# A gated unit over 8192 rows: eight neighbouring rows for a partition in groups of four tiles, in place of four in groups of two

## The chip, the cores and the metric

The kernel runs on one core of one Trainium2 chip. The metric is the device time of one execution in microseconds (us), with all inputs and outputs in the chip's memory (HBM); smaller is better. A core has 128 partitions of on-chip memory. Data come in and go out by DMA: a program's transfers are cut into packets, and 16 DMA engines work on these. In this kernel three engines compute: ScalarE (ACT in the profile), VectorE (DVE) and GpSimd (POOL). SyncE (SP) and ScalarE issue the transfers. TensorE does nothing. KB and MB of tiles and of distances in memory are counted here in powers of 1024, those of the profile's totals (268.44 MB) in powers of 1000.

## The reference

```python
def setup_inputs():
    return {
        "x": np.random.randn(8192, 8192).astype(np.float32),
    }

def reference(x: np.ndarray) -> np.ndarray:
    a, b = np.split(x, 2, axis=-1)
    return a * (1 / (1 + np.exp(-b)))
```

Each row of x holds 4096 values of a and then 4096 of b. The output row has the 4096 products of a and the sigmoid of b. A row of x takes 32 KB, a row of the output 16 KB. 268.44 MB are read and 134.22 MB written, and each byte is used once.

## The kernel before, in words

The 8192 rows are cut into 32 tiles of 256 rows; each of the 128 partitions holds R = 2 rows of a tile (64 KB of x, 32 KB of output). Lines 21 and 22 say which rows these are. With `"(g p h r) m -> g h p (r m)"` and h=2, a group g of two tiles covers 512 neighbouring rows; partition p takes four neighbouring rows of them, and tile h of the group gets two of the four. So the piece of x that a partition loads for one tile is 64 KB without a break, and the next partition's piece lies 128 KB further on (the other tile's 64 KB are between them). For the output the piece is 32 KB and the pitch from partition to partition 64 KB.

There are SLOTS = 2 input buffers `x_sb0`, `x_sb1` of 128 x 16384 float32 (8 MB each) and two output buffers `o_sb0`, `o_sb1` of 128 x 8192 float32 (4 MB each), used in turn: tile i uses slot i % 2. All instructions stand in program order on their engine (`place` keeps the waits that are needed and declares the others away):

- `load` (line 59) issues from SP's queue one transfer for the whole tile (line 63); for tile 0 there are two, a row each, `rows = [(0, 4), (4, 8)]`. A load into a slot waits for the products that read the slot two tiles before.
- `work` (line 72) does the sigmoid in place on ScalarE (line 82) and then the product of both halves (line 84), cut into two pieces for tiles 1 to 30: a part of 2 x 768 columns, whose product GpSimd makes (VectorE for tile 1), and a part of 2 x 3328 columns, whose product VectorE makes. Tiles 0 and 31 are done in four quarters on VectorE. For tiles 1 to 30 the sigmoid carries the wait for the output slot: it starts when the store of two tiles before has landed.
- `store` (line 66) issues from ScalarE's queue one transfer for the tile (line 68); tile 0 has two and tile 31 three.

The loop (lines 91 to 103) loads tiles 0 and 1 ahead; then for each tile it does the work, issues the load of tile i + 2 and the store of tile i. `_launch_early` moves the first load into the entry block, ahead of the barrier there, and `_close_on_sync` writes the end of the program by hand; the change does not touch these two.

The change touches lines 18 to 22 (the layout), 63 (in `load`) and 68 (in `store`), the only places that hold the group's size.

Of the kernel before, what the change touches and what calls it, by code (L numbers as in the profile page):

```python
# [8 lines left out]
def _tiles(ctx, tc, x, out):  # L9
    nc = tc.nc  # L10
    P = nc.NUM_PARTITIONS
    DEP = mybir.DependencyInfo(mybir.DependencyClass.Sync, mybir.DependencyReason.DATA)
    fp32 = mybir.dt.float32
    SIG = mybir.ActivationFunctionType.Sigmoid

    n_rows, n_cols = x.shape
    half = n_cols // 2
    R = 2
    SLOTS = 2
    n_tiles = n_rows // (P * R)  # L20
    x_g = x.rearrange("(g p h r) m -> g h p (r m)", p=P, h=2, r=R)
    out_g = out.rearrange("(g p h r) m -> g h p (r m)", p=P, h=2, r=R)

    pool = ctx.enter_context(tc.tile_pool(name="io", bufs=1))
    xs = [pool.tile([P, R * n_cols], fp32, name=f"x_sb{k}") for k in range(SLOTS)]
    os = [pool.tile([P, R * half], fp32, name=f"o_sb{k}") for k in range(SLOTS)]

    whole = [(0, 8)]
    rows = [(0, 4), (4, 8)]
    cut = half // 16 * 3  # L30
    few_and_most = [(0, 8, 0, cut), (0, 8, cut, half)]
    fourths = [(k, k + 2, k % 4 * half // 4, (k % 4 + 2) * half // 4) for k in range(0, 8, 2)]
    loads = [whole] * n_tiles
    works = [few_and_most] * n_tiles
    stores = [whole] * n_tiles
    behind = [0] * n_tiles
    loads[0] = stores[0] = rows
    works[0] = works[-1] = fourths
    stores[-1] = [(0, 4), (4, 6), (6, 8)]
    behind[-1] = 1  # L40

    def meet(a, b):
        return a[0] < b[1] and b[0] < a[1]

    traced = [[] for _ in range(SLOTS)]
    load_of, mul_of, store_of = {}, {}, {}

    def place(i, ins, *needs):


        kept = {n.ins.name for n in needs}
        for e in traced[i % SLOTS]:
            if e.ins.name not in kept:
                tc.declare_no_dep(ins.ins, e.ins, reason="follows from the waits that are kept")
        traced[i % SLOTS].append(ins)
        tc.keep_in_program_order(ins)
        return ins

    def load(i):
        for lo, hi in loads[i]:  # L60
            c = slice(lo * n_cols // 4, hi * n_cols // 4)
            free = [m for w, m in mul_of.get(i - SLOTS, []) if meet(w, (lo, hi))]
            ins = nc.sync.dma_start(out=xs[i % SLOTS][:, c], in_=x_g[i // 2, i % 2, :, c])  # L63
            load_of.setdefault(i, []).append(((lo, hi), place(i, ins, *free)))

    def store(i, lo, hi):
        c = slice(lo * half // 4, hi * half // 4)
        ins = nc.scalar.dma_start(out=out_g[i // 2, i % 2, :, c], in_=os[i % SLOTS][:, c])  # L68
        done = [m for w, m in mul_of[i] if meet(w, (lo, hi))]
        store_of.setdefault(i, []).append(((lo, hi), place(i, ins, *done)))  # L70

    def work(i, lo, hi, near, far):

        rows = xs[i % SLOTS].rearrange("p (r h m) -> p r h m", r=R, h=2)
        packed = os[i % SLOTS].rearrange("p (r m) -> p r m", r=R)
        r, c = slice(lo // 4, (hi + 3) // 4), slice(near, far)
        b = rows[:, r, 1, c]
        landed = [s for w, s in load_of[i] if meet(w, (lo, hi))]
        gone = [s for w, s in store_of.get(i - SLOTS, []) if meet(w, (lo, hi))]
        by_sigmoid = 0 < i < n_tiles - 1  # L80
        needs = [*landed, *(gone if by_sigmoid else ())]
        sig = place(i, nc.scalar.activation(out=b, in_=b, func=SIG), *needs)  # L82
        engine = nc.gpsimd if far == cut and i > 1 else nc.vector
        mul = engine.tensor_mul(out=packed[:, r, c], in0=rows[:, r, 0, c], in1=b)  # L84
        if by_sigmoid:
            for s in gone:
                tc.add_manual_dep(sig.ins, s.ins.name, DEP, reason="frees the output slot")
        place(i, mul, sig, *(() if by_sigmoid else gone))
        mul_of.setdefault(i, []).append(((lo, hi), mul))

    for i in range(SLOTS):
        load(i)
    for i in range(n_tiles):
        due = list(stores[i])
        for k, piece in enumerate(works[i]):
            work(i, *piece)
            ready = works[i][k - behind[i]][1] if k >= behind[i] else 0
            while len(stores[i]) > 1 and k < len(works[i]) - 1 and due[0][1] <= ready:
                store(i, *due.pop(0))
        if i + SLOTS < n_tiles:  # L100
            load(i + SLOTS)
        for lo, hi in due:
            store(i, lo, hi)
# [71 lines left out]
@with_exitstack  # L175
def kernel(
    ctx: ExitStack,
    tc: tile.TileContext,
    x: bass.AP,
    out: bass.AP,  # L180
):
    nc = tc.nc
    with ExitStack() as pools:
        _tiles(pools, tc, x, out)
    tc.close()
    tc.compile()
    _launch_early(nc)
    _close_on_sync(nc)
# [30 lines left out]
```

## Time and profile before

| What | Value |
|---|---|
| Median of 3 runs | 932.84 us (932.70 to 932.84) |
| Span of the profiled execution | 931.1 us |
| VectorE busy | 232.5 us (25%) |
| ScalarE busy | 229.8 us (25%) |
| GpSimd busy | 99.9 us (11%) |
| Packets of the load queue (q1) | 4752, 268.44 MB |
| Packets of the store queue (q10) | 5040, 134.22 MB |
| Whole-tile load, issue to landing | 43.5 us, median of 31 |
| Whole-tile store, issue to landing | 43.6 us, median of 30 |

How to read it: the span is the time between the first and the last thing that the profiler saw of one execution; the median is 1.7 us longer than it. An engine's busy time is the sum of its instructions' durations; a transfer's time to landing counts from its issue and so includes the time in which its packets stand behind others. A packet here is one partition's unbroken piece, so a whole-tile load has 128 packets of 64 KB and a whole-tile store 128 of 32 KB; besides these, each of the 33 loads and 35 stores has 16 packets of 4 bytes that report completion (33 x 144 = 4752 and 35 x 144 = 5040).

### The profile page before, as it was taken

To read this page: it belongs to the slowest core of one execution; us is meant where nothing else is said; L and a number is where in the kernel's file an instruction comes from. 1 tells how busy PE (TensorE), PEld (TensorE's weight loads), DVE (VectorE), ACT (ScalarE), POOL (GpSimd) and SP (SyncE) were. 2 spreads that over 40 slices of the span, in tenths; PEclk is the share of its full clock that TensorE was granted. 3 is DMA by queue.
4 is the path that set the end of the run, shared out by engine and by line. 5 is a ranking of instruction groups with operands and counts; after the bars stand their busy time and mean duration, and the time that the engine had idled before them with its cause. 6 is when DMAs were issued, how large, how long until landed. Compare 5 with 4: busy or idle time off the path is not lost.

```text
span 931.1 us, 325 instructions
## 1 busy us (share of the span) xinstructions
DVE 232.5 (25%) x39; ACT 229.8 (25%) x69; POOL 99.9 (11%) x33
## 2 busy tenths in 40 slices
DVE  1133311333113331133320333203332033320233
ACT  2123332033320333203332023320233302333023
POOL 0001111011110111101111011110111101111010
DMA  9999999999999999999999999999999999999998
GB/s 405 450 439 417 428 450 424 455 405 428 450 428 450 407 469 409 428 450 427 452 405 450 428 428 450 424 452 408 428 450 428 450 408 465 411 428 450 427 452 383
DMA packets 9793, 402.67 MB, mean 432 GB/s; under 512 B 1088, under 2 KB 1088, under 8 KB 1088
## 3 DMA queue, kind: packets, MB, share of 16 engines
q1 hardware_dynamic: 4752, 268.44, 66.6%
q10 hardware_dynamic: 5040, 134.22, 33.4%
q14 instruction: 1, 0.01, 0.0%
HBM read 268.44 MB, written 134.22 MB: 432 GB/s over the span
## 4 chain that ended last, share of the span: by engine, by line
DMA 75%; DVE 12%; ACT 12%; issue 0%; ACTq 0%; SPq 0%
DMA out_dram<-o_sb 65%; DVE o_sb L84 12%; ACT x_sb L82 12%; DMA x_sb<-in_x_dram 10%; ACTq L68 0%; SPq L63 0%
## 5 line engine op out<-in xcount | busy, mean ns | idle before, releaser
L84 DVE TENSOR_TENSOR o_sb<-x_sb 128x6656 f32<-128x6656 f32 (+2 forms) x39 | 232.5, 5970 | 690.2 <-ACT x_sb L82 690.2
L82 ACT ACTIVATE x_sb<-x_sb 128x1536 f32<-128x1536 f32 (+1 forms) x68 | 228.5, 3407 | 689.9 <-DMA out_dram<-o_sb 630.0
L84 POOL TENSOR_TENSOR o_sb<-x_sb 128x1536 f32<-128x1536 f32 x29 | 99.7, 3437 | 787.7 <-ACT x_sb L82 787.7
L82 ACT ACT_TABLE_LOAD x1 | 1.3, 1283 | 0.8 <-PEq L203 0.8
L203 POOL MEMSET const-float32-0.0<- 128x1 f32 x1 | 0.1, 98 | 0.2 <-issue 0.2
L203 POOL MEMSET const-bfloat16-1.0<- 128x1 bf16 x1 | 0.1, 101 | 0.0
L203 POOL MEMSET const-uint8-127<- 128x1 uint8 x1 | 0.1, 101 | 0.0
L203 POOL MEMSET const-float32-1.0<- 128x1 f32 x1 | 0.1, 98 | 0.0
## 6 DMA issues: line engine op xcount, KB each, us to landing
out_dram<-o_sb ACTq DMA_DIRECT2D x30, 4096.0 KB, 43.6
x_sb<-in_x_dram SPq DMA_DIRECT2D x2, 4096.0 KB, 16.4
out_dram<-o_sb ACTq DMA_DIRECT2D x3, 2048.0 KB, 28.0
out_dram<-o_sb ACTq DMA_DIRECT2D x2, 1024.0 KB, 8.3
x_sb<-in_x_dram SPq DMA_DIRECT2D x31, 43.5
```

The costliest lines, as they stand in the source:

```text
L82: sig = place(i, nc.scalar.activation(out=b, in_=b, func=SIG), *needs)
L84: mul = engine.tensor_mul(out=packed[:, r, c], in0=rows[:, r, 0, c], in1=b)
L203: nc = _bacc.Bacc("TRN2", target_bir_lowering=False, num_devices=1)
```

## The change

The group becomes H = 4 tiles of 1024 neighbouring rows. Partition p takes eight neighbouring rows of a group, and each of the four tiles gets two of them. A partition's piece of a tile stays as it was, 64 KB of x and 32 KB of output; the pitch from one partition's piece to the next one's grows from 128 KB to 256 KB for loads and from 64 KB to 128 KB for stores. 8 groups take the place of 16. Nothing else is edited: the buffers, the instructions, their shapes and their order on every engine are the same, and the same row of the output comes from the same row of x.

```diff
     R = 2
+    H = 4
     SLOTS = 2
     n_tiles = n_rows // (P * R)
-    x_g = x.rearrange("(g p h r) m -> g h p (r m)", p=P, h=2, r=R)
-    out_g = out.rearrange("(g p h r) m -> g h p (r m)", p=P, h=2, r=R)
+    x_g = x.rearrange("(g p h r) m -> g h p (r m)", p=P, h=H, r=R)
+    out_g = out.rearrange("(g p h r) m -> g h p (r m)", p=P, h=H, r=R)
...
-            ins = nc.sync.dma_start(out=xs[i % SLOTS][:, c], in_=x_g[i // 2, i % 2, :, c])
+            ins = nc.sync.dma_start(out=xs[i % SLOTS][:, c], in_=x_g[i // H, i % H, :, c])
...
-        ins = nc.scalar.dma_start(out=out_g[i // 2, i % 2, :, c], in_=os[i % SLOTS][:, c])
+        ins = nc.scalar.dma_start(out=out_g[i // H, i % H, :, c], in_=os[i % SLOTS][:, c])
```

## The prediction, made before the changed kernel ran

> **What bounds the kernel now.** I read the busy shares first, then the DMA's share stage by stage, then the chain of waits, and last the packet records, one for each packet with its queue, bytes, start and duration. The page's busy rows, its row of DMA shares and its queues:
>
> ```profile
> DVE 232.5 (25%) x39; ACT 229.8 (25%) x69; POOL 99.9 (11%) x33
> ...
> DMA  9999999999999999999999999999999999999998
> ...
> q1 hardware_dynamic: 4752, 268.44, 66.6%
> q10 hardware_dynamic: 5040, 134.22, 33.4%
> ```
>
> No computing engine is busy for more than a quarter of the span. The 16 DMA engines are busy in every slice, and the two queues' packets fill 66.6% + 33.4% = 100% of 16 engines' span. The windows by stage (columns: window, length, busy time of DVE, ACT and POOL, TensorE's clock, DMA share, GB/s):
>
> ```profile
> 46.00:104.00 58.00, 15.94 (x3) 18.59 (x6) 6.22 (x2) 1.00 0.98 425
> 104.00:395.00 291.00, 70.92 (x10) 71.90 (x21) 35.05 (x11) 1.00 1.00 434
> 395.00:627.00 232.00, 56.74 (x8) 57.11 (x17) 27.48 (x8) 1.00 1.00 434
> 627.00:860.00 233.00, 56.74 (x8) 57.98 (x17) 27.49 (x8) 1.00 1.00 433
> 860.00:912.00 52.00, 14.18 (x2) 8.43 (x4) 3.43 (x1) 1.00 1.01 435
> 912.00:931.10 19.10, 8.99 (x4) 7.08 (x4) 0.00 (x0) 1.00 0.94 403
> ```
>
> The rate is flat at 433 to 435 GB/s, and only the two ends fall below it. The chain of waits in order of time (start, length, what) repeats one cycle:
>
> ```profile
> 113.99 43.64 DMA out_dram<-o_sb
> 157.63 0.02 issue
> 157.66 7.13 ACT x_sb L82 x2
> 164.79 0.02 issue
> 164.81 7.10 DVE o_sb L84
> 171.91 0.02 issue
> 171.93 0.02 ACTq L68
> 171.95 0.04 issue
> 171.99 43.64 DMA out_dram<-o_sb
> ```
>
> A cycle is 171.99 - 113.99 = 58.00 us for two tiles, 2 x 12.58 MB (in millions of bytes; a third of it stores), so 25.17 / 58.00 = 434 GB/s. The chain names a store's landing, but those 43.64 us are mostly queueing, as the packet records show: on an engine packets of loads and stores alternate, a 64 KB load packet for 2418 ns, then a 32 KB store packet for 1213 ns. Eight pairs, the share of one engine in a tile, take 8 x 3.63 = 29.0 us, half the cycle; a store stands behind the one before it for the other 14.6 us. So the 14.2 us of ScalarE and VectorE in the cycle lie beside the other tile's packets, and what sets the time is how long an engine takes for a packet.
>
> The durations hardly vary: of the 3968 load packets of 64 KB, 120 take longer than 2418 ns, together 6.1 us on 16 engines, 0.38 us for each; of the 3840 store packets of 32 KB, 20 take longer than 1213 ns, the longest 1239. If memory at its present addresses held the engines back, these numbers would scatter.
>
> The sum for one engine: loads 248 x 2.418 + 16 x 1.213 = 619.1 us; stores 240 x 1.213 + 24 x 0.611 (16 KB) + 16 x 0.309 (8 KB) = 310.7 us; 929.8 us of packets. The first packet starts at 1.17 us and the last ends at 930.9 in a span of 931.1, which leaves 929.8 us for them: nothing is left over. The median of the runs, 932.84, is 1.7 us above the span, and I add that at the end.
>
> **The change, part by part.** *Instructions.* Built, the two kernels have the same instructions on every engine, in the same order, 35 on SP's queue and 35 products on VectorE: only line numbers differ. No wait is added, none is removed, no transfer passes another. Cost 0, and nothing needs to hide it.
>
> *Packets.* Each partition's piece stays unbroken: 64 KB of a load, 32 KB of a store. So the counts (248 + 16 and 240 + 24 + 16 for an engine) stay, and by the rows' durations the sum stays 929.8 us.
>
> *Addresses of the stores.* The pitch between partitions goes from 64 to 128 KB. No row shows a store at 128 KB; the nearest is the loads at 128 KB, 3848 of 3968 at their shortest duration. Upper bound: all 240 packets as slow as the slowest store, 1239 - 1213 = 26 ns, 6.2 us. Lower bound: 1212 is the shortest, 1 ns, -0.2 us. I take 0.
>
> *Addresses of the loads.* The pitch goes from 128 to 256 KB, which no row shows for any transfer. What a load packet costs when something does hold it back, two bursts of 16 packets near the start show, where the first stores join: at 21 us the median is 2612 ns (2481 to 2858), at 27.5 us it is 2460 ns. Upper bounds: 248 x (2612 - 2418) = 48 us and 248 x (2460 - 2418) = 10.4 us. Lower bound: the 0.38 us of late packets vanish. I take 0, since between 64 KB (stores) and 128 KB (loads) doubling shows no trend: both stand at one duration, at the same 27.1 GB/s for an engine (65,536 / 2418 ns and 32,768 / 1213 ns, 27.0).
>
> The Trainium skill has a rule against this change: "DMA: Bandwidth & Descriptors", section "Latency and other measured facts", row "HBM row pitch at large powers of two", gives for copies within HBM 207 GB/s at a pitch of 512 KiB, 164 at 2 MiB, 103 at 4 MiB, and 214 when 4 MiB is padded by 4 KiB. No run here shows a pitch of 512 KiB. If all packets slowed at 256 KB as that row does at 512, the estimate by the page would be 929.8 x 214 / 207 = 961 us of packets, 964 us in all; if the effect fades with halved pitch, as its figures do downwards, nothing is left.
>
> *Ends.* The first load's 16 packets take 1672 to 2022 ns in place of 1213, some 0.6 us once, and the end shows the engines finishing 0.3 us apart. Other addresses may shift these by some tenths either way.
>
> Sum: 0 + 0 + 0, with ends of -0.6 and +54 us (48 + 6.2). Span 931.1, time **932.8 us**.
>
> **The rivals.**
>
> *Loads are slowed by the wider pitch (slower, 0.24).* Place: the 64 KB packets of the load queue. It decides as soon as a packet takes 1.87 / 248 = 7.5 ns longer, 0.3%. For it: packets do lengthen in this trace when streams meet (the two bursts), so the engines' floor isn't far above what memory gives them; nothing shows 256 KB. Against: in the stages after the start, from 104 us on, 37 of 3552 load packets are late. Price by the milder burst, which is nearest to a steady state: 932.8 + 10.4 = 943 us; by the harsher 981. The skill's row named above is this mechanism.
>
> *Stores are slowed at 128 KB (slower, 0.02).* 932.8 + 6.2 = 939 us by the longest store. Against: loads run at that pitch at the floor.
>
> *The transfers are cut otherwise (slower, 0.02).* The step between partitions is now 65,536 elements for a load; should a transfer with it be cut into pieces of 16 KB, a load packet becomes 4 x 611 = 2444 ns, 26 more, 248 x 0.026 = 6.4 us, 939 us. Against: the built transfer has the same shape, 128 x 16384. Then the change would do something else than it says.
>
> *The start and the late packets improve (faster, 0.04).* All that the engines could give back: in the steady stage a load packet starts 2414 ns before the store packet behind it and that 1209 before the next, so records overlap by 4 ns, and 256 such pairs would be 927.5 us against the 929.8 of now. 2.3 us is the whole gain there can be, 930.5 us; for it stand the late first packets, against it that most of the 2.3 are completion packets and small last stores, which the change leaves alone.
>
> **How the numbers follow.** No change 0.68, slower loads 0.24, slower stores 0.02, other cutting 0.02, better start 0.04. What a measurement can tell from no change is 0.2%, 1.87 us. The three slower cases give 0.28 for slower; of the better start, a quarter stays below that bound, so 0.03 faster and 0.69 within. The range begins at 930.5, the whole possible gain. Upwards it must take in at least a third of the slower cases: the milder burst's 943 with 2 us for its scatter, 945. Above that lies half of the slow loads, 0.12.
>
> **What would show it.** Right: load packets still at 2418 ns and store packets at 1213, windows at 433 to 435 GB/s, a cycle of the chain of 58.0 us, stores landing in 43.6. Slow loads: q1's share of the engines above 66.6% with q10's at its old busy time, a cycle above 58.1 us. Slow stores: the same for q10. Other cutting: another number of packets than 4752 and 5040. Better start: the first window nearer to 46 us' worth of the flat rate, the later ones alike. The forecast is wrong if the flat rate falls below 433 GB/s: then memory, and not the engine, sets a packet's duration at the wider pitch.

## The result, and the profile after

The changed kernel takes 945.94 us (median of 15 runs, 932.69 to 951.95); the kernel before, beside it, 932.61 us (15 runs, 932.45 to 932.85). The ratio of the two is 1.0085 with a 95% interval of 1.0063 to 1.0106; it leaves out six of the 15 runs, those more than 1.5% above the fastest, which is one reason why it lies below the ratio of the medians. By the bound of 0.2% the change is slower.

The width of the range says more than the median. The 15 runs fall in three groups: one at 932.69, as before; three at 935.42 to 935.47; eleven from 942.73 to 951.95. The profiled execution, with a span of 944.6 us, is one of the eleven. Its queues on the page:

```profile
DMA packets 9793, 402.67 MB, mean 426 GB/s; under 512 B 1088, under 2 KB 1088, under 8 KB 1088
...
q1 hardware_dynamic: 4752, 268.44, 66.9%
q10 hardware_dynamic: 5040, 134.22, 33.0%
```

The packets are the same in number and bytes, so the transfers are cut as before. 66.9% of 944.6 is 631.9 us of load packets for an engine, where 66.6% of 931.1 was 620.1; the stores' 33.0% are 311.7, where they were 311.0. The loss sits in the load packets. The windows by stage of the changed kernel:

```profile
46.00:104.00 58.00, 15.94 (x3) 15.86 (x6) 3.48 (x2) 1.00 0.99 428
104.00:395.00 291.00, 70.92 (x10) 72.24 (x21) 35.35 (x11) 1.00 1.00 433
395.00:627.00 232.00, 56.73 (x8) 56.92 (x17) 27.41 (x9) 1.00 1.00 434
627.00:860.00 233.00, 56.74 (x8) 54.48 (x15) 26.55 (x8) 1.00 1.00 419
860.00:925.00 65.00, 14.18 (x2) 14.25 (x4) 6.85 (x2) 1.00 1.00 418
925.00:944.60 19.60, 8.99 (x4) 7.42 (x4) 0.00 (x0) 1.00 0.84 358
```

Until 627 us, with the wide pitch in every tile, the rate is the old 433 to 434 GB/s. Then it falls to 418 or 419 and stays there, though the addresses follow the same pattern as before that point. The last window, at a DMA share of 0.84, shows engines that end at different times. The chain of waits has the same story in its stores' landings (start, length):

```profile
116.73 43.65 DMA out_dram<-o_sb
...
174.74 43.64 DMA out_dram<-o_sb
...
580.73 43.73 DMA out_dram<-o_sb
...
638.82 45.36 DMA out_dram<-o_sb
...
698.54 46.09 DMA out_dram<-o_sb
...
758.99 46.00 DMA out_dram<-o_sb
...
819.35 46.01 DMA out_dram<-o_sb
```

The first of these starts 2.74 us later than its partner before (113.99), so something was lost at the start. From there to 580.73 eight cycles take (580.73 - 116.73) / 8 = 58.00 us each, the old length. From 638.82 on they take 59.72, 60.45 and 60.36. Of the 13.5 us between the spans, 2.5 are there by 580.73, 6.6 more come until 819.35, and the rest after.

The packet records name no engine, but each engine's packets follow one another without a gap, so an engine can be followed by joining each packet to the one that ends where it begins. "Behind" below is the start of an engine's load packet against the median of the 16. In the changed kernel the furthest engine is 549 ns behind at tile 1's first packet, 1809 at tile 2's, 2708 at tile 4's and still 2638 at tile 10's (from tile 2 on it is one engine, which had been 435 ns behind at tile 1); before, the furthest was 151, 360 and 298 ns behind at tiles 1, 2 and 4. Of the load packets of 64 KB that start between 100 and 600 us, 4 take longer than 2440 ns; of the 1328 that start after 610 us, 384 do, these with a median of 2901, and the late ones fall on all 16 engines alike (22 to 26 on each).

So there are two losses: an engine that slips some 2.7 us behind at the start (932.7 becomes 935.4 when nothing else happens), and, later, collisions of load packets (942 and more). The experiments ask what brings about each.

### The profile page after: what moved, and what is told of

Same layout as the page of the kernel before. It is cut to its first block, busy times and chain, and to the rows that moved or that the text cites. A ratio compares the mean times of both kernels' runs of the same rounds, so it can differ in the third digit from the quotient of the medians.

```text
span 944.6 us, 325 instructions
## 1 busy us (share of the span) xinstructions
DVE 232.5 (25%) x39; ACT 229.9 (24%) x69; POOL 99.9 (11%) x33
## 3 DMA queue, kind: packets, MB, share of 16 engines
q1 hardware_dynamic: 4752, 268.44, 66.9%
q10 hardware_dynamic: 5040, 134.22, 33.0%
## 4 chain that ended last, share of the span: by engine, by line
DMA 75%; DVE 12%; ACT 12%; issue 0%; ACTq 0%; SPq 0%
DMA out_dram<-o_sb 65%; DVE o_sb L85 12%; ACT x_sb L83 12%; DMA x_sb<-in_x_dram 10%; ACTq L69 0%; SPq L64 0%
```

## The experiments

The kernel before ran beside each set; its medians were 932.65 to 932.70 us. Three of its own runs in those sets stand out: 941.14 and 947.38 among the 23 beside e5 to e9, and 941.34 among the 22 beside e18 and e19. "At the floor" means below 934 us, "slipped" 934 to 937, "collided" 937 and above; the words go by the times, and what they stand for was seen in the profiled executions, three of which show collisions that begin late (the changed kernel, e14 and e16).

**Loads or stores: e1 and e2.** One pitch stays narrow.

```diff
 e1, against the changed kernel
-    out_g = out.rearrange("(g p h r) m -> g h p (r m)", p=P, h=H, r=R)
+    out_g = out.rearrange("(g p h r) m -> g h p (r m)", p=P, h=2, r=R)
...
+        ins = nc.scalar.dma_start(out=out_g[i // 2, i % 2, :, c], in_=os[i % SLOTS][:, c])
 e2: the same for x_g and the load
```

> Only the loads have the wide pitch (256 KB); the stores keep 64 KB, so the rows of the output stand in another order. If the wide pitch of the loads is the cause: as the changed kernel, a median of 942 to 950 us with a wide scatter from 932.7 up, load packets late (over 2440 ns) in the hundreds, store packets at 1213 ns. If the stores' pitch is the cause: 932.6 us, all runs within 0.3 us. If it takes both: between the two.

> Only the stores have the wide pitch (128 KB); the loads keep 128 KB, so the rows of the output stand in another order. If the loads' pitch is the cause: 932.6 us, all runs within 0.3 us, some 120 late load packets at the start and no more. If the stores' pitch is the cause: a median of 942 to 950 us with the scatter of the changed kernel.

Wide loads: median 935.53 us (932.56 to 950.82, 12 runs), 2 at the floor, 6 slipped, 4 collided; ratio 1.0054 (1.0024 to 1.0083). Wide stores: median 932.77 us (11 runs), 10 at the floor and one at 942.70; ratio 1.0010 (0.9993 to 1.0028). The slip comes with the loads. That fewer runs collided with narrow stores (4 of 12 against 11 of 15) isn't explained. It need not be the stores: the two counts come from different sets, the sets of the experiments ran on five chips, and the kernel before has collided runs in two of them only. So how often runs collide is best compared within a set: e1 with e2, e5 with e6, e15 with e17, e18 with e19. The profiled execution of e1 is a slipped one: one engine 2860 ns behind at tile 4, 2747 at tile 31, 2 load packets above 2440 ns after 100 us, and a last packet 1.7 us after the other engines'.

**The size of the pitch: e3, e4, e9 and e7.**

```diff
 against the changed kernel
-    H = 4
+    H = 8     (e3)   H = 1     (e4)   H = 32    (e9)
 e7
+    def odd(i):
+        lo = 960 * (i // H) + R * (i % H)
+        return x[lo : lo + 9 * P, :].rearrange("(p k) m -> p k m", k=9)[:, :R, :].rearrange("p r m -> p (r m)")
...
+            ins = nc.sync.dma_start(out=xs[i % SLOTS][:, c], in_=odd(i)[:, c])
```

> Groups of eight tiles, pitch 512 KB for loads and 256 KB for stores. If a load's pitch in powers of two sets how often packets collide: slower than the changed kernel, 950 to 1000 us, late load packets in every stage and not only after some tile. If only the one value 256 KB is bad: 932.6 us. If stores at 256 KB collide as loads do at 256 KB: late store packets too, of which there are 155 over 1217 ns in the changed kernel.

> No groups: a tile is one stretch of 256 rows, pitch 64 KB for loads and 32 KB for stores. If a wider pitch is what hurts, and the kernel before is at the engines' own rate: 932.6 us within 0.5. If instead the kernel before stands at a pitch that suits the memory and both neighbours are worse: 935 us or more, with late load packets.

> One group of all 32 tiles: pitch 2 MB for loads and 1 MB for stores. If collisions grow with a power-of-two pitch: late load packets from the first tile on and in every stage, and slower than 960 us. If a slip at the start and a chance of later collisions is all there is, whatever the pitch above 128 KB: 935 to 960 us, as with 512 KB.

> The loads have a pitch of 288 KB (nine rows) in place of 256, so they read other rows, some twice, and the output isn't the reference's; bytes, packets and stores are as in the changed kernel. If a pitch that is a power of two is what makes engines' streams meet in the memory: no slip, 932.7 to 933 us. If the distance alone does it: 935 us or more in most runs, as with 256 KB.

Pitch 64 KB (e4): 932.70 us, all 11 runs at the floor; ratio 1.0000 (0.9992 to 1.0009). Pitch 512 KB (e3): 935.86 us, none of 8 at the floor, 5 slipped, 3 collided, the worst 958.55; in its profile the rate is 432 to 435 GB/s in the same three windows from 104 to 860 us, and 148 load packets are above 2440 ns, 98 of them in the first 100 us, so the expected late packets in every stage did not come. Pitch 2 MB (e9): 1019.25 us (1002.99 to 1034.27, 6 runs), and here the rate itself is low from the start. The windows of e9:

```profile
104.00:395.00 291.00, 63.83 (x9) 68.59 (x20) 33.85 (x10) 1.00 1.00 415
395.00:627.00 232.00, 56.74 (x8) 52.48 (x15) 24.56 (x8) 1.00 1.00 404
627.00:860.00 233.00, 49.65 (x7) 49.86 (x14) 24.05 (x7) 1.00 1.00 399
```

1811 of its 3968 load packets take longer than 2440 ns. So at 2 MB the loads are slow in every stage, which at 256 and 512 KB they aren't (the stores' pitch grew too, to 1 MB, and no run parts the two). 288 KB (e7): median 932.69 us (932.39 to 951.81, 11 runs), 6 at the floor, 4 slipped, 1 collided. A pitch that isn't a power of two slips less often than 256 KB does, but it slips; the power of two isn't needed.

**Which tiles: e5, e6 and e14.** Tiles 0 to 3 cover the same 1024 rows in either layout, so the two can be joined there.

```diff
 e5, against the changed kernel (e6 and e14: "i >= 4" for "i < 4")
+    x_n = x.rearrange("(g p h r) m -> g h p (r m)", p=P, h=2, r=R)
+    out_n = out.rearrange("(g p h r) m -> g h p (r m)", p=P, h=2, r=R)
+    def at(wide, narrow, i):
+        return narrow[i // 2, i % 2] if i < 4 else wide[i // H, i % H]
...
+            ins = nc.sync.dma_start(out=xs[i % SLOTS][:, c], in_=at(x_g, x_n, i)[:, c])
...
+        ins = nc.scalar.dma_start(out=at(out_g, out_n, i)[:, c], in_=os[i % SLOTS][:, c])
```

> Tiles 0 to 3 (the first 1024 rows) keep the groups of two, pitch 128 and 64 KB; tiles 4 to 31 have the groups of four. If one engine slipping behind at the start, under the wide pitch, is what opens the way to the later collisions: no slip, load packets at 2418 ns to the end, 932.7 us with a scatter below 0.5 us. If the wide pitch makes packets collide by itself, at any time: a median of 940 us or more with the changed kernel's scatter.

> The reverse: tiles 0 to 3 have the groups of four, tiles 4 to 31 the groups of two. If the wide pitch only makes an engine slip at the start and the narrow one doesn't collide afterwards: most runs at 935.3 us (2.7 us for one engine that ends late), some at 932.7, none above 936. If an engine out of step is enough for collisions at any pitch: runs above 942 us too.

> The kernel with the wide start (tiles 0 to 3 in a group of four, tiles 4 to 31 in groups of two) a second time, for its profile and more runs. If a slipped engine is enough for collisions at the narrow pitch: again more than half of the runs above 940 us, and where the profile is one of those, load packets over 2440 ns in the stages after tile 4, whose pitch is narrow. If the narrow pitch doesn't collide: late packets only before tile 4, and the runs above 940 us stay without a place in the trace.

Narrow start, wide rest: 932.65 us, all 11 runs from 932.51 to 932.97; ratio 0.9995 (0.9980 to 1.0010). Wide start, narrow rest: 942.06 us (935.12 to 950.38, 6 runs), none at the floor, and again 941.70 us (935.20 to 954.84, 7 runs); 9 of the 13 collided. So the wide pitch does nothing in 28 of 32 tiles, and the collisions come at the narrow pitch too, against the first of e6's two expectations. The profile of e14 shows them. Its windows:

```profile
104.00:395.00 291.00, 70.92 (x10) 72.21 (x21) 35.33 (x11) 1.00 1.00 433
395.00:627.00 232.00, 56.73 (x8) 56.59 (x17) 27.09 (x9) 1.00 1.00 434
...
741.00:860.00 119.00, 28.36 (x4) 28.49 (x8) 13.74 (x4) 1.00 1.01 421
860.00:920.00 60.00, 14.19 (x2) 14.25 (x4) 6.87 (x2) 1.00 0.99 417
```

The same fall from 434 to 417 or 421 GB/s, this time after some 690 us and at the pitch of the kernel before. One engine was 2535 ns behind at tile 4; 290 of the 1328 load packets after 610 us take longer than 2440 ns.

**An engine put behind on purpose: e10, e11 and e12.**

```diff
 e10, against the kernel before (e12: against e5, with "i == 7")
+    late = pool.tile([P, 256], fp32, name="late")
...
             load(i + SLOTS)
+        if i == 1:
+            tc.keep_in_program_order(nc.sync.dma_start(out=late[:61, :256], in_=x[:61, :256]))
 e11: late[:128, :122] and x[:128, :122]
```

> The kernel before (pitch 128 and 64 KB throughout), and behind the load of tile 3 one small extra load of 61 partitions with 1 KB each, 62 KB that nothing reads, which should all fall to one DMA engine and put it some 2.5 to 4 us behind the other fifteen. If an engine out of step is enough for later collisions, at the narrow pitch too: most runs at 935 us or more, some above 941, load packets late in stages after that one. If the narrow pitch bears an engine out of step: every run at 932.7 plus the delay itself, 935 to 937 us, within 0.5 us.

> The control: the same extra 62 KB at the same place, but 128 partitions with 488 bytes each, so that all 16 engines take a share. All engines stay in step: 932.8 to 933.2 us under every theory that lays the loss on one engine out of step; 935 us or more if the extra load itself disturbs.

> The narrow start and then the wide groups (which alone took 932.65 us), and behind the load of tile 9 the same extra load on one engine. If an engine out of step is what the wide pitch needs to collide: 941 us or more in most runs. If the loss comes from the start alone: 935 to 937 us, as the delay itself.

e10 took 936.55 us (936.40 to 936.79), e12 936.52 us (936.21 to 936.76), e11, the control, 935.84 us (935.18 to 936.39), five runs each. The control lost nearly as much as the engine put behind (3.2 us against 3.9), so this doesn't show what it should. The packet records say why: on an engine a small packet takes turns with a 32 KB store packet (in e10 the first eight of the 61 start 1252 ns apart, and only when a store's packets are used up do they follow at 42 ns), so the extra load lets stores run ahead of loads and upsets their pairing, on one engine or on all. What can be kept: in the profiles of e10 and e12 one engine's load packets are 5.3 to 7.0 us behind the median from tile 12 on, while its store packets run ahead of the others', and none of the ten runs went above 936.8 us. So one engine far out of step is not enough for collisions.

**Which load: e13, e15, e16 and e17.**

```diff
 e13, against the kernel before
+    x_w = x.rearrange("(g p h r) m -> g h p (r m)", p=P, h=4, r=R)
...
+            ins = nc.sync.dma_start(out=xs[i % SLOTS][:, c], in_=(x_w[0, 1] if i == 1 else x_g[i // 2, i % 2])[:, c])
 e15: x_w[0, 0] if i == 0          e16: x_w[0, i] if i < 2
 e17, against the changed kernel, x_n with h=2
+            ins = nc.sync.dma_start(out=xs[i % SLOTS][:, c], in_=(x_n[0, 0] if i == 0 else x_g[i // H, i % H])[:, c])
```

> The kernel before, but the load of tile 1 alone has the pitch of 256 KB (it reads other rows, so tile 1 of the output isn't the reference's). In the changed kernel one engine fell 0.9 to 2.1 us behind between 36 and 49 us, in the last packets of tile 1's load and the first of tile 2's. If tile 1's load is where the slip starts: a good part of the runs at 935 us or more. If the slip needs the wide pitch in later loads too: 932.7 us in nearly all.

> The kernel before, with the pitch of 256 KB in tile 0's two loads alone (other rows, so tile 0 of the output isn't the reference's). If tile 0's load sets the engines apart and that alone makes one slip: runs at 935.3 and above 940 us. If the slip needs tile 1's load wide too: 932.6 us in all runs, but the engines 340 ns or more apart at the first packet of tile 1.

> The same with the loads of tiles 0 and 1 wide. If these two loads are what makes an engine slip: as the wide start, most runs at 935 us or more. If tiles 2 and 3 are needed: 932.6 us in nearly all.

> The changed kernel with the pitch of 128 KB in tile 0's two loads alone (other rows, so tile 0 of the output isn't the reference's). If tile 0's load is what sets the engines apart: no slip, 932.7 us in nearly all runs although 31 of 32 tiles are wide. If the loads from tile 1 on make an engine slip by themselves: 935 us or more in most runs, as in the changed kernel.

Tile 1 alone wide: 932.58 us, all 11 runs at the floor. Tile 0 alone wide: 936.58 us (935.18 to 951.79, 6 runs), none at the floor. Tiles 0 and 1: 935.41 us (932.78 to 945.85, 12 runs), 1 at the floor. And the changed kernel with a narrow tile 0, 31 of 32 tiles wide: 932.42 us, all 11 runs from 932.33 to 932.54; ratio 0.9998 (0.9989 to 1.0006). One load in 32 carries the whole effect. The windows of e17 show that the wide pitch runs at the rate of the kernel before from 104 to 860 us:

```profile
104.00:395.00 291.00, 70.93 (x10) 72.05 (x21) 35.16 (x11) 1.00 1.00 434
395.00:627.00 232.00, 56.74 (x8) 57.10 (x17) 27.50 (x9) 1.00 1.00 434
627.00:860.00 233.00, 56.74 (x8) 57.98 (x17) 27.50 (x8) 1.00 1.00 433
```

**Which packet of that load: e18 and e19.** Tile 0 comes in two transfers, a row of each partition in each.

```diff
 e18, against the kernel before, x_w as in e15 (e19: "lo > 0")
+            ins = nc.sync.dma_start(out=xs[i % SLOTS][:, c], in_=(x_w[0, 0] if i == 0 and lo == 0 else x_g[i // 2, i % 2])[:, c])
```

> The kernel before, with the pitch of 256 KB in the first of tile 0's two loads alone (row 0 of each partition; other rows, so that half of tile 0 of the output isn't the reference's). If the first packet of each engine sets how far apart the engines run: as with tile 0 wide, most runs at 935 us or more, the furthest engine 340 ns or more behind the median at tile 1's first packet. If it takes the whole tile: 932.6 us in nearly all.

> The same for the second of tile 0's two loads alone (row 1 of each partition). If the first packet of each engine decides: 932.6 us in all runs, the furthest engine under 300 ns behind. If it takes the whole tile, or the second transfer: 935 us or more in a part of the runs.

First transfer wide: 940.19 us (932.86 to 949.26, 11 runs), 1 at the floor, 3 slipped, 7 collided; ratio 1.0069 (1.0038 to 1.0101). Second transfer wide: 932.54 us, all 12 runs from 932.46 to 932.75. It is the first transfer, 128 packets of 32 KB in the first 12 us of the program.

The packet records of the profiled executions show what it leaves behind. Each engine's first packet, with nothing in flight but the 16 first ones, takes between some 1200 and 2240 ns, while nearly all later ones of tile 0 take 1211 to 1222 (at most 4 of 240 in an execution take longer, up to 1356). So the offsets between the engines, set by the start and the length of the first packet, stay nearly as they are to the last packet of tile 0 (561 ns become 549 in the changed kernel). How far the furthest engine is behind at its second packet, and how many of 16 are more than 300 ns behind, for one profiled execution of each kernel other than e9 to e12, beside all its runs:

| First transfer | Kernel | Furthest, ns | Over 300 ns | At the floor | Slipped | Collided |
|---|---|---|---|---|---|---|
| 64 KB | e4 | 240 | 0 | 11 | 0 | 0 |
| 128 KB | e2 | 145 | 0 | 10 | 0 | 1 |
| 128 KB | e5 | 218 | 0 | 11 | 0 | 0 |
| 128 KB | e13 | 207 | 0 | 11 | 0 | 0 |
| 128 KB | e17 | 261 | 0 | 11 | 0 | 0 |
| 128 KB | e19 | 153 | 0 | 12 | 0 | 0 |
| 288 KB | e7 | 364 | 1 | 6 | 4 | 1 |
| 256 KB | after | 561 | 5 | 1 | 3 | 11 |
| 256 KB | e1 | 451 | 4 | 2 | 6 | 4 |
| 256 KB | e6, e14 | 466, 532 | 3, 3 | 0 | 4 | 9 |
| 256 KB | e15 | 493 | 3 | 0 | 3 | 3 |
| 256 KB | e16 | 493 | 4 | 1 | 8 | 3 |
| 256 KB | e18 | 540 | 4 | 1 | 3 | 7 |
| 512 KB | e3 | 542 | 3 | 0 | 5 | 3 |

Taken together: with a first transfer at 256 KB 64 of 69 runs are above the floor, 37 of them collided. With one at 64 or 128 KB, 130 runs of the kernel before among them, 4 of 197 are, and all four collided. So a collision doesn't need a wide first transfer; the wide one makes it common.

Of the executions in the table, those that slipped have an engine 364 ns or more behind, those that didn't have none beyond 261. The line isn't that sharp: e10, whose extra load comes only behind the load of tile 3, starts at 128 KB with an engine 357 ns behind, and the furthest is 342 behind at tile 3, so nothing has slipped there. (e11 and e12 start with 206 and 188.) In the nine that slipped, one engine loses ground when stores have joined the loads (their first packets start at 23.6 to 24.0 us): some of its load packets of tiles 1 and 2 take up to 2.95 us in place of 2418 ns, it is 2.0 to 2.2 us behind at tile 3's first packet and 2.5 to 3.0 at tile 4's. It is one of the three furthest behind at tile 1's first packet (333 to 542 ns), but not always the furthest, so the offset alone doesn't say which engine slips.

## Why the prediction was wrong

*What bounds the kernel* held: the packets' durations on 16 engines set the time, 929.8 us of them before, and no computing engine came nearer to the bound.

*The instructions and the cutting* held: 4752 and 5040 packets, the same bytes.

*The stores' pitch* at 0 held: ratio 1.0010 (0.9993 to 1.0028) with e2, and its one collided run of 11 has its like in the kernel before.

*The loads' pitch* at 0 holds for the steady stages, which is what I argued it from: with e17 load packets at the wide pitch run at 434 GB/s, and the time is 932.42 us. The rival's picture, every load packet longer by the milder burst's 42 ns, is not what happened. Its 943 us lies near the measured 945.94 by accident: between 100 and 600 us four load packets are above 2440 ns, after 610 us 384 of 1328 are, by some 500 ns. The prediction's own sign of being wrong did come, a rate below 433 GB/s (419 after 627 us), but not for the reason given there: the rate falls as far at the narrow pitch in e14, and not at all at the wide pitch in e17.

*The ends* are the step that failed. I read the first load's packets, 1672 to 2022 ns in place of 1213, as 0.6 us spent once, and wrote that other addresses "may shift these by some tenths either way". They did shift by some tenths: the furthest engine went from 151 to 561 ns behind. I took such a shift as a term of the sum. It is a starting condition: it stays until the stores join, when one of the engines that are behind falls a further 2 us back (2.7 us of time when nothing else happens), and in 11 of 15 runs of the changed kernel collisions follow that cost 7 to 17 us more (942.73 to 951.95 against 935.4). e18 and e19 settle which transfer, e5 and e6 that it is the start.

The trace before held a sign that I left unread: I took "the engines finishing 0.3 us apart" as a detail of the end, and too small, for the last store packets of the 16 engines end 0.56 us apart. Between the first and the last engine there are 0.44 us at tile 1's first packet, 0.40 at tile 4's and, after one engine has lost 0.3 us in a gap at 367 us, 0.58 at tile 31's: nothing brings them together.

*The range* ended at 945, with half of the slow case's chance below it; the median lies 0.94 us above. The harsher burst of the same trace would have put the end at 981.

*The row on large powers of two* in the Trainium skill, "DMA: Bandwidth & Descriptors", section "Latency and other measured facts", agrees in kind with the 2 MB of e9 (1019.25 us, the loads late in every stage), and not with an estimate of 961 us of packets for its 512 KiB: e3 at 512 KB keeps 432 to 435 GB/s, and its loss is the slip.

What stays open: why a wide first transfer spreads the first packets (that it does, in the eight profiled executions at 256 or 512 KB, is shown; the reason in the memory isn't); which of the engines behind slips, and why it comes to rest near 2.7 us; and what starts the collisions, which also come, rarely, after a narrow first transfer. That the slip brings them on is not shown: they come with it, and one engine further behind in e10 and e12 brought none. That the offset of the first packets, and not some other trace of the first transfer, is the link between that transfer and the slip rests on the table above, since e10 to e12 did not give a clean test of an engine put behind.

## What to carry to other kernels

Where the DMA engines run without a gap, as here, nothing brought them back into step, so what the first few packets do can be worth more than their own duration: look at how far apart the engines are at the start, not only at the steady rate. A layout that costs in one transfer can be free in all others: e5 gives the first four tiles another pitch than the rest, computes the same output and stays at 932.65 us. Where runs of one kernel fall in groups, the groups are the finding, and a profile of one execution shows one of them.

## What the runs showed of the hardware beyond that

Offsets between DMA engines last: in e17 the furthest engine is 379 ns behind at tile 2 and 380 at tile 11, over 256 us of packets. In the changed kernel's profile the collisions keep a place: after 690 us some 150 of the 284 late load packets are the third or the seventh of an engine's eight packets of a tile, and fewer than ten the first or the fifth. In e14 they don't: each of the eight places has 24 to 51 of its 288. And the queues take turns by packets, not by bytes: in e10 one 1 KB load packet (46 ns) after the other waited out a 32 KB store packet (1213 ns), seven times in a row.
